# A hybrid attention and DeltaNet layer: five tiles of one merge gate instead of two behind the last heads, two fewer at the end of the attention

## The chip, the cores and the metric

The kernel runs on one NeuronCore of a Trainium2 chip. The metric is device time in microseconds (us) of one execution, smaller is better. The core's engines each work through a queue of their own: TensorE (PE in the profile; its weight loads are PEld), VectorE (DVE), ScalarE (ACT), GpSimd (POOL), and SyncE (SP), which here issues nearly all DMAs.

## The reference

One decoder layer on 512 tokens of width 2048. A normalised and modulated input `h` is projected to everything else; two branches work side by side, and a gated sum of both goes through the output projection:

```python
h = rms_norm(x, norm_w) * (1.0 + scale) + shift
proj = h @ w_in
aq, ak, av, ag, d_qkv, dz, db, da, mg_a, mg_b = jnp.split(proj, _split_points(), axis=-1)
...
a_out = swa_attention(aq, ak, av, sinks).astype(x.dtype) * jax.nn.silu(ag)
y_a = a_out @ w_o_swa
...
o = gated_delta_rule(dq, dk, dv, g, beta)
o = rms_norm(o, dn_norm_w) * jax.nn.silu(dz.reshape(B, T, DN_V_HEADS, DN_HEAD_V).astype(f32))
y_b = o.reshape(B, T, DN_VAL).astype(x.dtype) @ w_o_dn
y = jax.nn.sigmoid(mg_a) * y_a + jax.nn.sigmoid(mg_b) * y_b
return x + gate * (y @ w_out)
```

The attention has 32 query heads of 64 in 4 groups, a window of 128 and attention sinks. The DeltaNet has 32 value heads in 16 groups of two. The change is about `mg_a`, the merge gate of the attention branch: 2048 channels, which are 16 tiles of 128 channels by 512 tokens.

## The kernel before

Everything is float32, and each large product is made of three matmuls: both operands are split into a high part (`hh`, `whi`) and a low part (`hl`, `wlo`), and `mm3` (L272 to L277) adds high x high, low x high and high x low. `hh` and `hl` hold `h`, 16 tiles of 128 x 512 each, for nearly the whole program.

A *channel tile* (`channel_tile`) is one product of 128 output channels: 16 steps of three matmuls, 48 in all, over weights of 1 MB. The weights come in by an order written out by hand, `plan`: a list of jobs, one a tile, whose loads SP issues into two raw buffers (`raw`; a third for part of the time). Each raw tile is split in two halves by ScalarE (`whi`, L53) and VectorE (`wlo`, L54) into three pairs of buffers. The code must use the tiles in just the order of the list, so a tile moved in the code is moved in `plan` too.

A *merge gate* (`merge_gate`) is a channel tile, a tanh on ScalarE (`mth`, L298) and a store by SP to `ma_d` (L301). It hangs on nothing but `h`, so it can stand anywhere up to the output projection of the attention, which reads `ma_d`.

The work that hangs on long chains (a group of DeltaNet heads, a group of attention heads) is written as generators. They stand in a list `live`; every second step of a channel tile calls `pump`, which lets each generator go on when its count of pumps has run out. So the small matmuls of such a chain stand between matmuls of channel tiles, eight pumps to a tile. What is left when no tile follows is run out by `drain_live`, with nothing between.

The stages that the change touches:

- *DeltaNet heads* (`deltanet`): 16 groups, five channel tiles each. Behind the last group its scan is still in flight: four chunks one after the other (`pp`, `pv`, `pd`, `po`), then on VectorE the norm (`roy`, and `osb` at L1077), transposes `pto` on TensorE (L309), the product with the gate `zh` (L1086), stores and sums to `oq_d`. Merge gates follow, and `drain_live`.
- *DeltaNet output projection* (`branch_b`): seven products `od` of 2048 x 1024 weights, made of `oraw` tiles that are loaded from `oq_d` and split to `oh` and `ol`. Merge gates stand in front of it and behind it.
- *Attention* (`attention`): four groups of eight channel tiles, then merge gates. Each group of heads has four blocks of 128 tokens, one after the other: scores `S` (two groups of matmuls, L1413), mask and maxima on VectorE (L1419, L1424 to L1432), exponentials on ScalarE (L1437), normalisation on VectorE (L1445), transposes `pP` and copies `pT`, the product with the values `O` (L1464), the gate (`ao`, L1471) and, behind the last block of a group, a store to `ao_d`. The last group's chain runs into the merge gates.
- *Attention output projection* (`finish`): 16 channel tiles `os`. Its input takes the place of `h`: each of 16 tiles of `ao_d` is loaded by SP to `aoraw` (eight buffers, shared with the queries `aq`) and split to `hh` (ScalarE, L53) and `hl` (VectorE, L54), once the last merge gate has read that part of `h`.

The build puts each engine's instructions in a fixed order, which need not be the order of the code. An engine goes through its instructions in that order.

Of the kernel before, what the change touches and what calls it, by code (L numbers as in the profile page):

```python
# [19 lines left out]
KT = D // P  # L20
# [17 lines left out]
class Layer:  # L38
# [149 lines left out]
    def plan(self):  # L188
        a, jobs = self.a, []
        wi = lambda name, t: jobs.append((name, a["w_ch"][t]))  # L190
        jobs += [(f"st{u}", a["w_st"][u]) for u in range(KT // 2)]
        for j in range(NFIRST):
            wi(f"mb{j}", 96 + j)
        for kind, j in self.mixed():
            wi(f"{kind}{j}", (16 if kind == "k" else 96) + j)
        ma = lambda r: [wi(f"ma{j}", 146 + j) for j in r]
        ma(range(0, 3))
        for g in range(KH):
            wi(f"q{g}", g)
            for e in (2 * g, 2 * g + 1):  # L200
                wi(f"v{e}", 32 + e)
            for e in (2 * g, 2 * g + 1):
                wi(f"z{e}", 64 + e)
        ma(range(3, 5))
        ma(range(5, 7))
        for m, (name, _, w) in enumerate(self.od_order()):
            src = a["w_od"][w] if w else self.od_d[name]
            jobs += [(f"od{m}_{b}", src[b]) for b in range(8)]
        ma(range(7, 9))
        for t in range(2):  # L210
            wi(f"ak{t}", 128 + t)
        for n in range(4):
            for j in range(4):
                wi(f"aq{4 * n + j}", 112 + 4 * n + j)
            for j in range(4):
                wi(f"ag{4 * n + j}", 130 + 4 * n + j)
        ma(range(9, 16))
        jobs += [(f"os{j}", a["w_os"][j]) for j in range(KT)]
        self.jobs = jobs

# [405 lines left out]
    def deltanet(self):  # L626
# [10 lines left out]
        with ExitStack() as ps:  # L637
# [35 lines left out]
            with ExitStack() as sb:  # L673
                wk = sb.enter_context(tc.tile_pool(name="dnB", bufs=2, reuse_waits="tile"))
                self.tt = []
                for n in range(4):
                    t = wk.tile([P, NTB, P], F32, tag=f"tt{n}", name=f"tt{n}", bufs=1)
                    nc.gpsimd.memset(t[HD:P, :, 0:HD], 0.0)
                    self.tt.append(t)
                self.wmore = sb.enter_context(tc.tile_pool(name="wmore", bufs=1, reuse_waits="tile"))  # L680
                self.load_job()
                for g in range(KH):
                    if g == KH - 1:
                        self.wmore = None
                    if g == 2:
                        self.beside(self.ordered(self.od_sums()), 0.13, "ws")
                    if g == 8:
                        self.drain_slow(s1)
                        es1.close()
                        late = ps.enter_context(tc.tile_pool(name="late", bufs=1, side="right", reuse_waits="tile"))  # L690
                        self.beside(self.ordered(self.gate(late)), 0.125, "gate")
                    self.heads(wk, g)
                for j in range(3, 5):
                    self.merge_gate("ma", j, self.ma_d)
                self.drain_live()
                self.drain("ws")
                self.drain("gate")
# [419 lines left out]
    def branch_b(self):  # L1117
        tc, nc, a = self.tc, self.nc, self.a
        with ExitStack() as es:
# [14 lines left out]
            def split(u):  # L1134
                if u < 56:
                    parts[u] = [wk.tile([P, 2, 256], F32R, tag="o" + x, name="o" + x, bufs=8) for x in "hl"]
                    self.split(*parts[u], raws.pop(u))
                    load(u + 4)
# [27 lines left out]
            for j in range(3):  # L1166
                for u in (2 * j, 2 * j + 1):
                    split(u)
                if j < 2:
                    self.merge_gate("ma", 5 + j, self.ma_d)  # L1170
            for m, (name, _, _) in enumerate(order):
                ps = {}
                for kt in range(KT):
# [15 lines left out]
                    self.half_done()  # L1189
                    if kt % 2:  # L1190
                        del parts[u]
            for j in range(7, 9):
                self.merge_gate("ma", j, self.ma_d)
            self.drain_live()

# [70 lines left out]
    def attention(self):  # L1266
        tc, nc, a = self.tc, self.nc, self.a
        with ExitStack() as es:
# [33 lines left out]
                self.go(self.key_pair(wk, t, self.channel_tile(f"ak{t}"), blk, kw, kd), 0)  # L1302
            for n in range(4):
                self.group(wk, kd[n], n, blk, mask, sink, qw)
            for j in range(9, KT):
                self.merge_gate("ma", j, self.ma_d)
            self.drain("ws")
            self.drain_live()
# [466 lines left out]
```

## Time and profile before

| | us |
|---|---|
| median of 3 runs (2883.14 to 2886.53) | 2885.73 |
| the profiled execution | 2886.63 |
| its span, first to last instruction | 2884.9 |
| TensorE busy in the span | 2832.8 |
| VectorE busy | 1857.8 |
| ScalarE busy | 1139.0 |
| GpSimd busy | 272.5 |

In the profile a row of a timeline has the start (us from the span's start), the duration, the engine, the line, the operation, what it writes and reads (out<-in), the shape and the count; in brackets stands how long the engine was idle before it, and for what. Matmuls overlap, so the distance from start to start tells their pace, not the duration. In the view of waits a row has the total, the times and the longest. A row of the view by stretches gives the stretch, its length, the busy time of PE, PEld, DVE, ACT and POOL (with the count of instructions), the granted TensorE clock as a share of full speed, the DMA share and GB/s. In the chain of waits a row is the start, the duration and the work.

### The profile page before, as it was taken

How to read it: one execution, taken by the hardware profiler on the slowest of the kernel's cores; microseconds unless marked ns; L12 is line 12 of the kernel's file. 1: busy time of each engine (PE TensorE's matmuls, PEld its weight loads, DVE VectorE, ACT ScalarE, POOL GpSimd, SP SyncE). 2: the span in 40 equal slices, each digit the busy share in tenths (PEclk: the TensorE clock that was granted, in tenths of full speed). 3: DMA queues.
4: the chain of work that ended last, by engine and by line, in shares of the span. 5: the costliest groups of instructions: out<-in, count | busy, mean ns of one | idle time of the engine just before them, and what ended most of it. 6: DMA issues, size and time to landing. Idle time of an engine off the chain costs nothing.

```text
span 2884.9 us, 38287 instructions
## 1 busy us (share of the span) xinstructions
PE 2832.8 (98%) x14428; PEld 2329.4 (81%) x14428; DVE 1857.8 (64%) x3020; ACT 1139.0 (39%) x2161; POOL 272.5 (9%) x266
## 2 busy tenths in 40 slices
PE   8899999999999999999999999999999999999999
PEld 6677888888888888888887788888887788788787
DVE  6765899777776555566665456665556655554565
ACT  4354333433334333333333344443344434432343
POOL 0012121101111111111100000000100100000000
PEclk9999999999999999999999999999999999999999
DMA  9756554636767877878873477675745547365575
GB/s 381 290 171 195 180 172 156 210 109 199 226 178 216 236 227 230 260 230 242 252 202 97 133 247 265 241 252 202 224 148 163 166 147 219 119 226 181 187 237 164
DMA packets 205729, 590.08 MB, mean 205 GB/s; under 512 B 74821, under 2 KB 99909, under 8 KB 154345
## 3 DMA queue, kind: packets, MB, share of 16 engines
q1 hardware_dynamic: 195336, 529.44, 53.8%
q0 software_dynamic: 10208, 58.20, 10.4%
q8 instruction: 113, 1.85, 0.3%
q14 instruction: 72, 0.58, 0.1%
HBM read 523.79 MB, written 166.40 MB: 239 GB/s over the span
## 4 chain that ended last, share of the span: by engine, by line
PE 87%; DVE 2%; issue 2%; DMA 1%; ACT 0%; SPq 0%; POOL 0%; DVEq 0%; POOLq 0%; ACTq 0%
PE mm L275 21%; PE mm L277 20%; PE mm L276 20%; PE od L276 3%; PE od L275 3%; PE od L277 3%; PE m L276 2%; PE m L277 2%; PE m L275 2%; PE S L1413 1%; PE po L1045 1%; PE O L1464 1%; PE pv L1026 1%; PE pP L309 1%; PE po L1044 1%
## 5 line engine op out<-in xcount | busy, mean ns | idle before, releaser
L275 PE MATMUL mm<-hh,whi 128*128 128x512 f32 x2784 | 1127.4, 405 | 2.3 <-ACT whi L53 1.6
L277 PE MATMUL mm<-hh,wlo 128*128 128x512 f32 x2784 | 1089.7, 391 | 1.1 <-DVE wlo L54 1.1
L276 PE MATMUL mm<-hl,whi 128*128 128x512 f32 x2784 | 1088.8, 391 | 0.0
L54 DVE TENSOR_TENSOR wlo<-raw,whi 128x1024 fp32r<-128x1024 f32 (+1 forms) x476 | 588.8, 1240 | 464.5 <-ACT whi L53 458.5
L53 ACT CAST whi<-raw 128x1024 fp32r<-128x1024 f32 (+1 forms) x476 | 495.8, 1045 | 786.0 <-PE mm L276 665.3
L275 PEld LDWEIGHTS mm<-hh,whi 128*128 128x128 f32 x2784 | 524.6, 188 | 115.6 <-issue 9.6
L277 PEld LDWEIGHTS mm<-hh,wlo 128*128 128x128 f32 x2784 | 523.7, 188 | 114.4 <-DVE wlo L54 1.9
L276 PEld LDWEIGHTS mm<-hl,whi 128*128 128x128 f32 x2784 | 525.1, 189 | 101.8 <-issue 1.4
L276 PE MATMUL od<-wlo,oh 128*128 128x512 f32 x448 | 174.6, 390 | 0.8 <-DVE wlo L54 0.8
L275 PE MATMUL od<-whi,oh 128*128 128x512 f32 x448 | 174.9, 391 | 0.3 <-ACT whi L53 0.3
L277 PE MATMUL od<-whi,ol 128*128 128x512 f32 x448 | 174.4, 389 | 0.0
L813 POOL TENSOR_TENSOR E<-E,neg_g 128x512 f32<-128x512 f32 x64 | 79.8, 1248 | 946.6 <-DMA E<-g_rows 721.1
L865 DVE TENSOR_TENSOR A<-A,atmp 128x62 f32<-128x62 f32 (+30 forms) x124 | 112.0, 903 | 1.6
L858 DVE TENSOR_TENSOR atmp<-A 128x62 f32<-128x62 f32 (+30 forms) x124 | 110.3, 890 | 1.3
L276 PEld LDWEIGHTS od<-wlo,oh 128*128 128x128 f32 x448 | 84.1, 188 | 18.1 <-DVE wlo L54 1.1
L275 PEld LDWEIGHTS od<-whi,oh 128*128 128x128 f32 x448 | 84.1, 188 | 17.8 <-ACT whi L53 0.7
L277 PEld LDWEIGHTS od<-whi,ol 128*128 128x128 f32 x448 | 84.1, 188 | 17.7
L54 DVE TENSOR_TENSOR wlo<-raww,whi 128x1024 fp32r<-128x1024 f32 x56 | 68.4, 1222 | 44.3 <-ACT whi L53 44.3
L53 ACT CAST whi<-raww 128x1024 fp32r<-128x1024 f32 x56 | 58.9, 1054 | 79.4 <-PE m L277 71.8
L972 POOL TENSOR_TENSOR qe<-qe,yq 128x512 f32<-128x512 f32 x32 | 47.3, 1497 | 410.3 <-DMA qe<-eg_rows 346.8
L1047 ACT COPY osb<-po 128x256 f32<-128x256 f32 x64 | 23.8, 372 | 148.2 <-PE po L1045 148.2
L1437 ACT ACTIVATE sm<-sm,mx,rs 128x256 f32<-128x256 f32 (+1 forms) x128 | 71.7, 561 | 3.3 <-DVE mx L1432 3.3
(341 smaller groups left out, 3261.0 us busy)
## 6 DMA issues: line engine op xcount, KB each, us to landing
raw<-in_w_ch SPq DMA_DIRECT2D x158, 1024.0 KB
wa<-in_w_ada_ss SPq DMA_DIRECT2D x32, 1024.0 KB
od_m<-in_w_od POOLq DMA_DIRECT2D x32, 1024.0 KB, 10.7
raw<-od_m SPq DMA_DIRECT2D x32, 1024.0 KB
raw<-in_w_od SPq DMA_DIRECT2D x24, 1024.0 KB
E<-g_rows SPq DMA_DIRECT2D x64, 256.0 KB
od_m<-in_w_od SPq DMA_DIRECT2D x16, 1024.0 KB
od_m<-od_m SPq DMA_DIRECT2D x16, 1024.0 KB
```

The costliest lines, as they stand in the source:

```text
L53: self.nc.scalar.copy(out=hi, in_=src)
L54: self.nc.vector.tensor_tensor(out=lo, in0=src, in1=hi.bitcast(F32), op=ALU.subtract)
L275: nc.tensor.matmul(ps, lhsT=wh, rhs=xh, start=first, stop=False)
L276: nc.tensor.matmul(ps, lhsT=wh, rhs=xl, start=False, stop=False)
L277: self.last_mm = nc.tensor.matmul(ps, lhsT=wl, rhs=xh, start=False, stop=last).ins
L309: self.small = self.nc.tensor.transpose(dst[:, c * P : (c + 1) * P], src_cols(c), self.ident).ins.name
L813: self.in_turn(nc.gpsimd.tensor_tensor(out=E, in0=E, in1=ng, op=ALU.add))
L858: eng.tensor_tensor(out=t, in0=A[:, m : m + 1, m + 1 :].to_broadcast([P, m, n]), in1=A[:, :m, m : m + 1].to_broadcast([P, m, n]), op=ALU.mult,
L865: eng.tensor_tensor(out=A[:, :m, m + 1 :], in0=A[:, :m, m + 1 :], in1=t, op=ALU.add)
L972: self.in_turn(nc.gpsimd.tensor_tensor(out=qf, in0=qf, in1=q, op=ALU.mult))
L1026: nc.tensor.matmul(pv[:, e, :], lhsT=TT[e][:, c, :], rhs=r[:, e, :] if c else v[e][:, c, :], start=True, stop=True)
L1437: nc.scalar.activation(t, t, AF.Exp, scale=r[:, h : h + 1], bias=mx[:, h : h + 1], accum_out=den[:, h : h + 1])
```

## The change

The 16 tiles of the gate are spread otherwise over the program:

| place | tiles before | tiles after |
|---|---|---|
| in the DeltaNet's first part | 0, 1, 2 | 0, 1, 2 |
| behind the last group of heads | 3, 4 | 3 to 7 |
| in front of the DeltaNet output projection | 5, 6 | 8 |
| behind it | 7, 8 | 9, 10 |
| at the end of the attention | 9 to 15 | 11 to 15 |

In `plan` the jobs of the weights move in the same way. No work is added or left out.

```diff
@@ plan
-        ma(range(3, 5))
-        ma(range(5, 7))
+        ma(range(3, 9))
         for m, (name, _, w) in enumerate(self.od_order()):
...
-        ma(range(7, 9))
+        ma(range(9, 11))
...
-        ma(range(9, 16))
+        ma(range(11, 16))
@@ deltanet
                     self.heads(wk, g)
-                for j in range(3, 5):
+                for j in range(3, 8):
                     self.merge_gate("ma", j, self.ma_d)
                 self.drain_live()
@@ branch_b
-                if j < 2:
-                    self.merge_gate("ma", 5 + j, self.ma_d)
+                if j == 1:
+                    self.merge_gate("ma", 8, self.ma_d)
...
-            for j in range(7, 9):
+            for j in range(9, 11):
                 self.merge_gate("ma", j, self.ma_d)
             self.drain_live()
@@ attention
-            for j in range(9, KT):
+            for j in range(11, KT):
                 self.merge_gate("ma", j, self.ma_d)
```

What this does to the order on the engines is seen at two places. The lines of the changed kernel have numbers that are one lower from `plan` on.

Behind the last group of heads, VectorE before: `osb` is the norm in front of the transposes `pto`, `zh` the product that reads them, `E` the sums that are stored, `wlo` a half of weights, `ol` a part of the input of `od`.

```order
L1077 TENSOR_TENSOR osb<-osb,roy 128x512 x2
L1086 TENSOR_TENSOR zh<-pto,zh 128x512 x2
L1110 TENSOR_TENSOR E<-zh 128x256
L1106 TENSOR_TENSOR E<-zh 128x256
L1107 SCALAR_TENSOR_TENSOR E<-E,zh 128x256
L1111 SCALAR_TENSOR_TENSOR E<-E,zh 128x256
L54 TENSOR_TENSOR wlo<-raw,whi 128x1024
L54 TENSOR_TENSOR ol<-oraw,oh 128x512 x4
```

And VectorE with the change:

```order
L1076 TENSOR_TENSOR osb<-osb,roy 128x512 x2
L54 TENSOR_TENSOR wlo<-raw,whi 128x1024
L1085 TENSOR_TENSOR zh<-pto,zh 128x512 x2
L54 TENSOR_TENSOR wlo<-raw,whi 128x1024 x3
L1105 TENSOR_TENSOR E<-zh 128x256
L1106 SCALAR_TENSOR_TENSOR E<-E,zh 128x256
L1109 TENSOR_TENSOR E<-zh 128x256
L1110 SCALAR_TENSOR_TENSOR E<-E,zh 128x256
L54 TENSOR_TENSOR wlo<-raw,whi 128x1024 x2
L54 TENSOR_TENSOR ol<-oraw,oh 128x512
```

Weights of gates that were not there now stand between the norm, the product and the sums. On TensorE, 6 matmuls of a gate stand between the last scan step `po` and `pto` before, and 54 now; between `pto` and the first `od` stand 96 before and 144 now. On SP, the first four `oraw` loads stand in front of the store of the first gate that follows `pto` before, and now behind the store of gate 7.

At the end of the attention, ScalarE before: `es` and `sm` are the exponentials of the last block, `pT` copies, `mth` the tanh of a merge gate (the last one shown is that of gate 15), `hh` the high parts of the output projection's input.

```order
L1431 ACTIVATE es<-es 128x8
L1437 ACTIVATE sm,den<-sm,mx,rs 128x256 x8
L298 ACTIVATE mth<-mm 128x512
L53 CAST whi<-raw 128x1024 x2
L1455 COPY pT<-pP 128x512 x2
L53 CAST whi<-raw 128x1024
L298 ACTIVATE mth<-mm 128x512
L53 CAST hh<-aoraw 128x512 x7
L53 CAST whi<-raw 128x1024
L53 CAST hh<-aoraw 128x512 x7
L298 ACTIVATE mth<-mm 128x512
```

And ScalarE with the change (again the last `mth` is that of gate 15):

```order
L297 ACTIVATE mth<-mm 128x512
L53 CAST hh<-aoraw 128x512 x7
L53 CAST whi<-raw 128x1024
L53 CAST hh<-aoraw 128x512 x5
L1430 ACTIVATE es<-es 128x8
L1436 ACTIVATE sm,den<-sm,mx,rs 128x256 x8
L297 ACTIVATE mth<-mm 128x512
L53 CAST whi<-raw 128x1024
L1454 COPY pT<-pP 128x512 x2
L53 CAST whi<-raw 128x1024
L53 CAST hh<-aoraw 128x512 x4
```

The exponentials of the last block stood two gates ahead of the first `hh`; now twelve `hh` stand ahead of them, and the tanh of gate 15 stands behind them. On VectorE, with the change, four `hl` stand between the masks of the last block's first and second scores, and six among and behind the steps of its maxima:

```order
L54 TENSOR_TENSOR hl<-aoraw,hh 128x512 x4
L1418 TENSOR_TENSOR sm<-S,mask 128x512 x2
L1423 TENSOR_REDUCE mx<-sm 128x2 x2
L54 TENSOR_TENSOR hl<-aoraw,hh 128x512
L1426 TENSOR_TENSOR mx<-mx,rs 128x8
L54 TENSOR_TENSOR hl<-aoraw,hh 128x512
L1427 TENSOR_TENSOR mx<-mx,sink 128x8
L54 TENSOR_TENSOR hl<-aoraw,hh 128x512
L1429 TENSOR_TENSOR es<-sink,mx 128x8
L54 TENSOR_TENSOR hl<-aoraw,hh 128x512
L1431 TENSOR_SCALAR mx<-mx 128x8
L54 TENSOR_TENSOR hl<-aoraw,hh 128x512 x2
```

Before, all sixteen `hl` stand behind `ao` of the last block. On TensorE, between the second scores of the last block and its first transposes `pP`, stand 54 matmuls before (30 of gate 13 and 24 of gate 14), and a whole further gate, 48 matmuls, stands behind `O`; now 30 of gate 15 and one of the output projection stand between them. Between that matmul and `O` stand four more, one is within `O`, and behind `O` stand 30 that read the twelve tiles already split. On SP, eight `aoraw` loads stand behind the store of gate 14, then a load of weights, the store of gate 15, and only then the stores of the last group and the four loads that read them; before, the last eight loads stand behind those stores.

## The prediction

> **What bounds the kernel now.** I read the page's busy line and chain first, then the view of who waited for whom on TensorE, then the timelines around the two places where the change adds and takes cover.
>
> ```profile
> PE 2832.8 (98%) x14428; PEld 2329.4 (81%) x14428; DVE 1857.8 (64%) x3020; ACT 1139.0 (39%) x2161; POOL 272.5 (9%) x266
> PE 87%; DVE 2%; issue 2%; DMA 1%; ACT 0%; SPq 0%; POOL 0%; DVEq 0%; POOLq 0%; ACTq 0%
> ...
> PE v L275 <- ACT hh L469: 18.7, 14, 3.3
> PE pd L1041 <- DVE vs L1033: 5.7, 3, 2.5
> PE pto L309 <- DVE osb L1077: 3.7, 1, 3.7
> PE mm L275 <- ACT mth L298: 0.7, 1, 0.7
> ```
>
> TensorE is busy for 98% and makes 87% of the chain, so a merge gate costs its matmuls wherever it stands: a tile moved is worth only the TensorE waits that it covers or lays bare. In all waits there is one at each place the change touches: 3.7 us for `pto`, behind the last group of heads, and 0.7 us for `mth`, between the last merge gate and the first tile of the output projection. The sum is made against the profiled execution, 2886.63 us (its span 2884.9); the median of the runs, 2885.73, lies 0.9 below, and the forecast is given on the median.
>
> **The three tiles that move behind the heads.** TensorE there, before:
>
> ```profile
> 1635.62 0.40 PE L277 MATMUL mm<-hh,wlo 128*128 128x512 f32 x1
> 1639.75 1.32 PE L309 MATMUL pto<-ident,osb 128*128 128x128 f32 x8 [3.73 <-DVE osb L1077]
> ...
> 1641.73 0.63 PE L277 MATMUL mm<-hh,wlo 128*128 128x512 f32 x1
> 1642.15 0.63 PE L275 MATMUL mm<-hh,whi 128*128 128x512 f32 x1
> ...
> 1645.47 0.39 PE L276 MATMUL mm<-hl,whi 128*128 128x512 f32 x1
> 1645.70 0.40 PE L277 MATMUL mm<-hh,wlo 128*128 128x512 f32 x1
> ...
> 1640.93:1644.34 3.41, 3.41 (x11) 2.67 (x10) 2.39 (x6) 0.00 (x0) 0.00 (x0) 0.50 0.48 161
> 1647.75:1651.16 3.41, 3.41 (x16) 2.81 (x15) 2.11 (x3) 2.79 (x5) 0.00 (x0) 1.00 0.81 287
> ```
>
> With two gates, the transposes of the last heads stand 6 matmuls behind the last scan step and wait 3.73 us for VectorE to scale `osb`. Soon after, the granted clock is 0.50 for one stretch of 3.41 us: matmuls start 0.42 us apart there, and 0.23 us apart later. Eight start where fifteen would, so the stretch loses 7 x 0.23 = 1.6 us. In the new order 54 matmuls stand there, 12 us of work against a wait of under 4, so both go: **-3.7 and -1.6 us**. The gain's bounds are 3.7 (if the clock falls there anyway) and 5.3; I take 5.3, since nothing else idles there.
>
> The cover for the loads of the DeltaNet output projection gets thinner, because their issues on SP now stand behind the store of gate 7 and only gate 8 (48 matmuls, 11 us) is left in front of the first `od` tile:
>
> ```profile
> 1643.89 3.54 SPq L1132 DMA_DIRECT2D oraw<-oq_d  x4
> 1648.92 1.66 ACT L53 CAST oh<-oraw 128x512 fp32r<-128x512 f32 x3
> ```
>
> From the first issue to the first cast took 5.0 us there, which with 0.6 for a cast and 0.7 for its low part is under 7 us. Eleven cover it; I cost it at nothing. The two gates behind that projection stay two. The moved weight loads and gate stores are as many as before, one of each per tile.
>
> **The two tiles fewer at the end of the attention.** Here the order matters more than the count. Let s be the start of the second group of score matmuls of the last block.
>
> ```profile
> 2514.02 1.14 PE L1413 MATMUL S<-kd,aq 64*128 64x256 f32 x8
> 2515.09 0.50 PE L275 MATMUL mm<-hh,whi 128*128 128x512 f32 x1
> 2527.46 1.03 PE L309 MATMUL pP<-ident,sm 128*128 128x128 f32 x8
> 2534.79 1.97 PE L1464 MATMUL O<-pT,vtok_a 128*64 128x128 f32 x32
> 2548.60 0.50 PE L275 MATMUL mm<-hh,whi 128*128 128x512 f32 x1 [0.75 <-ACT mth L298]
> ...
> 2519.52 0.60 ACT L1437 ACTIVATE sm<-sm,mx,rs 128x256 f32<-128x256 f32 x1
> 2523.63 0.59 ACT L1437 ACTIVATE sm<-sm,mx,rs 128x256 f32<-128x256 f32 x1
> 2524.21 0.58 ACT L298 ACTIVATE mth<-mm 128x512 f32<-128x512 f32 x1
> 2537.68 4.71 ACT L53 CAST hh<-aoraw 128x512 fp32r<-128x512 f32 x7 [1.42 <-PE mm L277]
> 2542.30 1.05 ACT L53 CAST whi<-raw 128x1024 fp32r<-128x1024 f32 x1
> 2543.25 2.87 ACT L53 CAST hh<-aoraw 128x512 fp32r<-128x512 f32 x5
> ...
> 2515.18 1.29 DVE L1419 TENSOR_TENSOR sm<-S,mask 128x512 f32<-128x512 f32 x2 [1.53 <-PE S L1413]
> 2516.39 1.27 DVE L1424 TENSOR_REDUCE mx<-sm 128x2 f32<-128x512 f32 x2
> 2517.69 0.17 DVE L1427 TENSOR_TENSOR mx<-mx,rs 128x8 f32<-128x8 f32 x1
> 2524.78 2.19 DVE L1445 TENSOR_SCALAR sm<-sm,den 128x256 f32<-128x256 f32 x8
> 2526.89 1.22 DVE L54 TENSOR_TENSOR wlo<-raw,whi 128x1024 fp32r<-128x1024 f32 x1
> 2528.09 0.69 DVE L1457 COPY pT<-pP 128x512 f32<-128x512 f32 x1
> 2536.93 0.68 DVE L1471 TENSOR_TENSOR ao<-O,sg 128x512 f32<-128x512 f32 x1
> 2538.34 4.79 DVE L54 TENSOR_TENSOR hl<-aoraw,hh 128x512 fp32r<-128x512 f32 x7 [0.72 <-ACT hh L53]
> ...
> 2514.79 0.79 SPq L1312 DMA_DIRECT2D aoraw<-ao_d  x2
> 2680.94 2.00 DMA y_d<-m
> 648.03 3.60 DMA E<-g_rows
> ```
>
> Before, 54 matmuls (12.4 us, 0.229 each) lie between s+1.07 and the first transposes `pP` at s+13.4, and a whole further gate lies behind `O`. Now gate 15, the last, is under way at s: 30 of its matmuls follow, it ends at s+1.07+6.9 = s+8.0, and next in TensorE's order come one matmul of the output projection, `pP`, and `O`. The last block's softmax is bare, and it starts later, because ScalarE and VectorE now split twelve of the sixteen `aoraw` tiles ahead of it:
>
> 1. The seventh tile's buffer is one that this second group of scores reads; its load was issued at 2514.79, s+0.8. No row has that load's landing. The nearest 256 KB ones took 2.0 us (`y_d`, a store) and 3.6 (`E`, a load); I take 2.7, about midway: s+3.5.
> 2. ScalarE then casts tile 7 (0.6), one half of weights (1.05) and five tiles (2.87), and ends at s+8.0.
> 3. VectorE does masks and maxima of the first scores (4 us ahead of s), four `hl` (4 x 0.69), the masks and maxima of the second (2.5) by s+4.9, then four `hl` with four 0.17 us steps of the maxima among them (3.5): s+8.4. So the exponentials start at s+8.5, not at s+5.5 (2519.52).
> 4. They take 4.7 (2519.52 to 2524.21); the tanh of gate 15 stands behind them, 0.6: s+13.8. The first matmul of the output projection waits for that tanh, as it does at 2548.60. TensorE idles from s+8.0 to s+13.85: **5.9 us**.
> 5. The normalised `sm` were ready 7.45 us after the exponentials began (2519.52 to 2526.97): s+15.95, `pP` done at s+16.4, where without waiting it would be at s+15.0: **1.4 us**. Four matmuls later (s+17.3) the second `pP` waits until VectorE has done a `wlo` (1.22) and a copy of `pT` (0.69), about s+18.0: **0.7 us**. `O` waits for the last copies, **0.4 us**, and ends near s+21.
>
> Together 8.4 us; with the load at 2.0 or 3.6 in step 1 it is 7.7 or 9.3. Behind `O`: `ao` (0.7), a store (2.0), a load (2.7), `hh` (0.6) and `hl` (0.7) give 6.7 us, or 7.6 with the slower load, against 32 matmuls (7.3 us) that need none of it. I take **0.3 us**, bounds 0 and 2.1 (if the store too takes a load's 3.6). The 0.75 us wait of before goes: its place is inside the 5.9.
>
> The clock: an idle of 3.73 us cost one half-speed stretch above, and 5.9 will cost at least one. It falls into the restart, where about 2.3 us of TensorE work double and 1.1 us of the waits of step 5 take part of it up: **1.2 us**; bounds 0.4 (the stretch lies nearly all in the idle time) and 3.3 (two dense stretches). The Trainium skill, page "TensorE: Matmul & The Clock Gate", Part 1 on the clock gate, says that the clock halves after an idle window of about 3.4 us that runs free of the kernel, and returns only after a busy one. The 3.41 us row above agrees with that length, and by that rule the broken restart could hold the half clock longer: the total would be 2892.4 us (worked out at the second rival) where one stretch as in the row gives 2889.5.
>
> **The sum:** -3.7 - 1.6 + 8.4 + 0.3 + 1.2 - 0.75 = +3.8 us, so 2885.73 + 3.8 = **2889.5 us** (2890.4 in a profiled execution). With all bounds at their low end +1.9, at their high end +8.6.
>
> The order in the places that carry this is shown with the change. What can be told from no change is about 0.2%, 5.8 us: the three runs alone spread over 3.4 us.
>
> **The rivals.**
> - *The last group of heads comes too late for the output projection* (slower). Place: its tile 12, the first that needs `ao` of group 3. For it speaks that store and load follow each other with no other gate behind `O`; against it that the queue carries little else then. It decides once the round trip takes 1.9 us more than the 32 matmuls. At 2.1 us that bubble has a stretch of half clock of its own, 1.6 us less the 0.3 already counted: 2889.5 + 3.4 = 2892.9 us.
> - *The clock stays halved through the restart* (slower). From s+13.85 to s+21 TensorE has 5.0 us of work; doubled, less 2.5 us of waits, it adds 2.5 in place of 1.2, and one dense stretch more adds 1.6: 2892.4 us. For it speaks that the restart stops three times; against it that at 1640.93 one stretch sufficed, but work was dense there.
> - *The relief behind the heads is given back in front of `od`* (slower). If the twelve first `oraw` loads crowd each other past the 11 us, the 3 us would return: 2892.5 us. The 7 us above speak against it.
> - *The softmax is hidden after all* (faster). If the five remaining tiles cover it, only -5.3 and at most -0.75 remain: 2879.7 us. The 12.4 us that lie there before and are 6.9 now speak against it.
> - That the change moves nothing is excluded by the order.
>
> **How the numbers follow.** My forecast 0.50; late group 0.22; halved clock 0.17; relief given back 0.05; hidden softmax 0.06. Slower by over 0.2% is the three middle ones, 0.44; within 0.2% 0.50; faster 0.06. The forecast's own range is 2887.5 to 2891.5. The range of 8 in 10 takes in the bounds of the sum (+1.9 to +8.6) and a little of the faster side: 2885 to 2895.
>
> **What would show it.** The wait of `pto` for `osb` and the 0.50 stretch behind it are gone; a wait of some 6 us of the first `os` matmul for `mth` appears, with waits of `pP` and `pT` of about 1.4 and 0.7 behind it and a stretch at 0.50; exponentials of the last block start some 8.5 us after the second scores; no wait of over 1 us in front of `od`. The prediction is wrong if the first `os` matmul waits under 3 us, or if new waits outside these two places come to more than 2 us.

## The result, and the profile after

| | before | with the change |
|---|---|---|
| median (us) | 2883.62 (2879.43 to 2887.36, 22 runs) | 2887.99 (2883.65 to 2891.35, 22 runs) |
| ratio, 95% interval | | 1.0013 (1.0007 to 1.0019) |
| profiled execution, span | 2886.63, 2884.9 | 2891.35, 2889.6 |

The change costs 0.13% of 2883.62, that is 3.8 us (2.0 to 5.5 by the interval; the two medians differ by 4.4): within the 0.2% that was called no change, and by the amount that was forecast. The parts behind that amount were not all as forecast. Both profiled executions lie 3 us or more above their kernel's median.

The page of the changed kernel, busy line and chain:

```profile
PE 2832.5 (98%) x14428; PEld 2328.2 (81%) x14428; DVE 1858.2 (64%) x3020; ACT 1139.1 (39%) x2161; POOL 275.2 (10%) x266
PE 86%; DVE 2%; issue 2%; DMA 2%; ACT 1%; POOL 0%; SPq 0%; DVEq 0%; POOLq 0%; ACTq 0%
```

The busy time of TensorE is that of before (2832.8), so all of the difference is in what it waits for. The view of who waited for whom on TensorE:

```profile
PE mm L274 <- ACT mth L297: 5.7, 2, 4.3
...
PE od L275 <- DVE wlo L54: 2.4, 1, 2.4
...
PE pP L308 <- DVE sm L1444: 0.3, 1, 0.3
```

The row of `pto` is gone. Waiting for `mth` has grown from 0.7 us in one place to 5.7 in two, and the od row is new. The timeline of TensorE at the four places:

```profile
1632.49 0.39 PE L1044 MATMUL po<-vn,E 128*128 128x128 f32 x2
1645.01 1.03 PE L308 MATMUL pto<-ident,osb 128*128 128x128 f32 x8
...
1919.42 0.59 PE L275 MATMUL od<-wlo,oh 128*128 128x512 f32 x1 [2.36 <-DVE wlo L54]
...
2018.76 0.50 PE L274 MATMUL mm<-hh,whi 128*128 128x512 f32 x1 [1.41 <-ACT mth L297]
...
2533.48 1.13 PE L1412 MATMUL S<-kd,aq 64*128 64x256 f32 x8
2545.97 0.79 PE L274 MATMUL mm<-hh,whi 128*128 128x512 f32 x1 [4.34 <-ACT mth L297]
2546.56 2.23 PE L308 MATMUL pP<-ident,sm 128*128 128x128 f32 x8
2550.30 1.45 PE L308 MATMUL pP<-ident,sm 128*128 128x128 f32 x8
2552.49 1.75 PE L1463 MATMUL O<-pT,vtok_a 128*64 128x128 f32 x28
```

`pto` now has no wait. The first matmul of the output projection waits 4.34 us. The 1.41 us at 2018.76 are in front of `ak0`, the first tile of the attention, and the 2.36 us are inside the DeltaNet output projection. Neither of the last two was in the forecast.

A stop costs about 0.3 us more than the time in its brackets. Matmuls of 0.39 us start 0.23 us apart when nothing holds them, so that 0.16 us of overlap is lost at a stop, and the second matmul behind it starts 0.34 us after the first (2018.76 and 2019.10).

To see what each place is worth, the program is cut at six starts on TensorE: the last `po`, the first and the last `od`, the first `S`, the second scores of the last block (s), and the last `mm` (the end of the attention's output projection).

| start at (us) | last po | first od | last od | first S | s | last mm | span |
|---|---|---|---|---|---|---|---|
| before | 1634.36 | 1664.31 | 1975.98 | 2079.25 | 2514.02 | 2722.59 | 2884.9 |
| with the change | 1632.61 | 1678.54 | 1993.32 | 2098.29 | 2533.48 | 2726.79 | 2889.6 |
| heads_alone (below) | 1630.23 | 1654.40 | 1966.09 | 2071.06 | 2506.50 | 2715.07 | 2877.7 |

A tile takes 10.88 us: between the last `po` and the first `od` the changed kernel has six and heads_alone four, and (45.93 - 24.17) / 2 = 10.88. Taking 10.88 for every tile that moved into or out of a stretch, the difference to the kernel before is, for all profiled executions:

| us | up to last po | heads (po to od) | od | od to S | S to s | end (s to last mm) |
|---|---|---|---|---|---|---|
| with the change | -1.8 | -5.8 | +3.1 | +1.7 | +0.4 | +6.5 |
| heads_alone | -4.1 | -5.8 | 0.0 | +1.7 | +0.7 | 0.0 |
| end_alone | -3.5 | 0.0 | +0.1 | 0.0 | +1.4 | +6.8 |
| two_in_front | -6.8 | -5.8 | -0.2 | 0.0 | +1.9 | +6.4 |
| other_bank | -0.7 | -5.8 | -0.3 | +1.7 | +1.0 | +5.9 |
| skipped_buffer | -1.5 | -5.8 | +0.2 | +1.8 | +0.2 | +6.1 |
| late_splits | -4.1 | -5.8 | -0.4 | +1.7 | +2.0 | +6.8 |
| all_late | -6.6 | -5.8 | -0.7 | +1.7 | +0.7 | +2.6 |
| six_at_end | -6.9 | -5.8 | +0.3 | 0.0 | +0.6 | +2.3 |
| four_at_end | -2.1 | -5.8 | -0.4 | 0.0 | +1.0 | +13.1 |
| none_behind | -1.8 | -5.8 | +0.3 | +10.0 | +2.5 | 0.0 |

The first column is a part of the program in which nothing was moved, and it differs by up to 6.9 us from one execution to the next. The stretch from the first `S` to s has the same order on TensorE in nearly all these kernels and still differs by up to 2.0 us (in none_behind it has a wait of its own, below; in four_at_end 18 matmuls of gates stand behind s instead of ahead of it, and are taken into account). Behind the last `mm` each took 0.2 to 1.1 us longer than the kernel before did. So one profile's span says little about a change of 4 us, and the times below are medians of many runs, while the columns tell where the time goes. What belongs to the change is -5.8, +1.7 and +6.5, together +2.4 us; the executions below with the same order at the end put the last term at 5.9 to 6.8.

### The profile page after: what moved, and what is told of

Its sections match the earlier page's. It is cut to its first block, busy times and chain, and to the rows that moved or that the text cites. A ratio compares the mean times of both kernels' runs of the same rounds, so it can differ in the third digit from the quotient of the medians.

```text
span 2889.6 us, 38283 instructions
## 1 busy us (share of the span) xinstructions
PE 2832.5 (98%) x14428; PEld 2328.2 (81%) x14428; DVE 1858.2 (64%) x3020; ACT 1139.1 (39%) x2161; POOL 275.2 (10%) x266
## 3 DMA queue, kind: packets, MB, share of 16 engines
q8 instruction: 113, 1.85, 0.3%
## 4 chain that ended last, share of the span: by engine, by line
PE 86%; DVE 2%; issue 2%; DMA 2%; ACT 1%; POOL 0%; SPq 0%; DVEq 0%; POOLq 0%; ACTq 0%
PE mm L274 20%; PE mm L276 20%; PE mm L275 20%; PE od L275 3%; PE od L276 3%; PE od L274 3%; PE m L275 2%; PE m L276 2%; PE m L274 2%; PE S L1412 1%; PE po L1044 1%; PE pP L308 1%; PE pv L1025 1%; PE O L1463 1%; PE po L1043 1%
```

## The experiments

All spread the thirteen movable tiles otherwise, or change one thing in the changed kernel. "3, 1, 2, 7" are the tiles behind the last heads, in front of the DeltaNet output projection, behind it, and at the end of the attention; the kernel before is 2, 2, 2, 7 and the change 5, 1, 2, 5. Unless one says so, the order of the weights' loads follows.

### Each half of the change alone

heads_alone, 3, 1, 2, 7 (against the changed kernel):

```diff
-                for j in range(3, 8):
+                for j in range(3, 6):
-                    self.merge_gate("ma", 8, self.ma_d)
+                    self.merge_gate("ma", 6, self.ma_d)
-            for j in range(9, 11):
+            for j in range(7, 9):
-            for j in range(11, KT):
+            for j in range(9, KT):
```

> The change's half at the heads alone: three tiles behind the last heads, one in front of the DeltaNet output projection, two behind it, seven at the end as in the kernel before. Theory 'the heads' gain is real': no wait of pto for osb, no half-clock stretch behind it, 5.3 us less than the kernel before from these two. If the wait of the first attention tile ak0 for mth (1.4 us in the changed kernel) comes from the count of tiles in front of it, it is here again, since the count between heads and attention is that of the changed kernel, and the net is about -4 us. Rival 'the gain is taken back in the output projection': the wait of od for wlo (2.4 us, 4 with its half-clock stretch) is here too, the net is about 0. In the last block the order is that of before: first os matmul waits about 0.75 us.

end_alone, 2, 2, 4, 5: the loops at the heads and in front of `od` as in the kernel before, `range(7, 11)` behind it, `range(11, KT)` at the end.

> The change's half at the end of the attention alone: two and two tiles around the heads as in the kernel before, four behind the DeltaNet output projection, five at the end. Theory 'the bare softmax costs it': pto waits 3.7 us with its half-clock stretch as before, the first os matmul waits 4.3 to 5.9 us for mth, the whole 6.5 (by the changed kernel's trace) to 9.2 us (by the prediction's sum) slower than the kernel before. Rival 'the loss lies elsewhere, in od and ak0': at most 4 us slower. No wait of ak0, if that hangs on the count of tiles in front of it (34 here, 31 in the changed kernel).

Measured: heads_alone 2879.57 us against 2885.5 before, ratio 0.9983 (0.9974 to 0.9991), 4.9 us less; end_alone 2891.72, ratio 1.0023 (1.0013 to 1.0033), 6.6 us more. Together they make +1.7, the change +3.8: the intervals of each part are 2 to 3 us to either side, and the sum lies inside them. TensorE in heads_alone, the last `po` and the first `od`, with as many tiles between them as before:

```profile
1630.11 0.39 PE L1044 MATMUL po<-vn,E 128*128 128x128 f32 x2
...
1654.40 0.39 PE L274 MATMUL od<-whi,oh 128*128 128x512 f32 x1
```

And the same two in the kernel before:

```profile
1634.25 0.39 PE L1045 MATMUL po<-vn,E 128*128 128x128 f32 x2
...
1664.31 0.39 PE L275 MATMUL od<-whi,oh 128*128 128x512 f32 x1
```

30.06 us before and 24.29 here: 5.8 us, the wait of `pto` (3.73), what a stop costs beyond that, and the half-clock stretch behind it (1.6). The same 5.8 stand in every execution that has three or more tiles behind the heads. The gain at the heads is real, and the loss is at the end of the attention. heads_alone also has the wait of `ak0` (1.41 us), and no long wait of `od` (0.97); its time is below both kernels.

### What od and ak0 wait for

two_in_front, 4, 2, 2, 5: `range(3, 7)` behind the heads, gates 7 and 8 in front of `od`.

> The changed kernel with four tiles behind the heads and two in front of the DeltaNet output projection, in place of five and one. TensorE's order is the same, instruction by instruction; what differs is which PSUM buffer each tile has and when the oraw tiles are loaded and split. Theory 'ak0 waits because its PSUM buffer is that of the last gate': the wait of 1.4 us goes. If the wait of od for wlo (2.4 us) is due to the split order in front of od, it goes as well: together 1.5 to 5.5 us less than the changed kernel; if it is an accident of one execution, only 1.4. Rival 'neither hangs on this': the time of the changed kernel, within 1 us. The end of the attention as in the changed kernel.

other_bank:

```diff
-            self.pmm = es.enter_context(tc.tile_pool(name="pmma", bufs=2, space=PSUM, reuse_waits="tile"))
+            self.pmm = es.enter_context(tc.tile_pool(name="pmma", bufs=2, space=PSUM, reuse_waits="tile")); self.pmm.tile([P, T], F32, tag="mm", name="skip")
```

> The changed kernel, every engine's order the same, but one PSUM buffer of the attention's pool is given out and not used, so that each tile there takes the other of the two buffers: ak0 not that of the last gate in front of it, and the first tile of the output projection not that of gate 15. Theory 'the softmax chain sets the end, the tanh only shows it': the wait of ak0 goes (1.4 us), the first os matmul doesn't wait for mth, but the transposes pP right behind it wait about 4.3 us for sm instead; 1 to 2 us less than the changed kernel. Rival 'the tanh that stands behind the exponentials is the cause': the 4.3 us go as well, and 5 to 7 us are gained with the clock's stretches.

In other_bank the buffer that was given out and not used came back at once: in the built program every tile of it has the PSUM buffer that it has in the changed kernel. So it answers nothing about buffers, and is a second look at the changed kernel: 2886.75 us, ratio 1.0012 (1.0003 to 1.0020), a wait of `od` of 0.94 us in place of 2.36, and the same waits at the other places. The 3.1 us in `od` are thus an accident of the one profiled execution; none of the eleven others has them. VectorE, in the changed kernel:

```profile
1917.55 0.69 DVE L1213 SCALAR_TENSOR_TENSOR yb<-bth,pty 128x512 f32<-128x512 f32 x1 [5.47 <-DMA yb_d<-yb]
```

The halves of weights `wlo` that `od` waits for stand right behind this `yb`, and it waited 5.47 us for a store of an earlier `yb`, where the eleven others wait 3.3 to 4.3 us. That execution lies 3.4 us above its kernel's median.

two_in_front: 2887.49 us, ratio 1.0009 (1.0000 to 1.0018). The wait of `ak0` is gone, as expected, and the end costs what it did. The time to the changed kernel differs by less than the intervals tell apart.

To move the buffers in earnest, skipped_buffer writes the skipped buffer once:

```diff
             self.pmm = es.enter_context(tc.tile_pool(name="pmma", bufs=2, space=PSUM, reuse_waits="tile"))
+            skip = self.pmm.tile([P, T], F32, tag="mm", name="skip")
+            nc.tensor.transpose(skip[:, 0:P], self.ident, self.ident)
```

> The changed kernel with one transpose of 128x128 into a PSUM buffer of the attention's pool ahead of its first tile, never read, so that every tile there takes the other of the two buffers; the orders else are the same, but for one half of weights on ScalarE and VectorE near ak0. Theory 'the softmax chain sets the end, the tanh only shows it': the wait of ak0 (1.4 us) is gone, and the first os matmul no longer waits for mth (4.3 us), but pP, one matmul behind it, waits about 4.4 us for sm; 1 to 2 us less than the changed kernel. Rival 'the tanh behind the exponentials is the cause': the 4.3 us go too, 5 to 7 us less.

Measured 2886.82 us, ratio 1.0012 (1.0003 to 1.0021): as slow as the change. Its waits on TensorE:

```profile
PE pP L308 <- DVE sm L1446: 4.7, 2, 4.5
...
PE skip L1270 <- ACT mth L297: 1.4, 1, 1.4
```

Both waits have changed their owner. The 1.4 us in front of `ak0` now belong to the transpose that took `ak0`'s buffer, so it is the buffer that waits, and whoever comes first to it. In the built program the last gate behind `od` has PSUM buffer 0, that of `ak0`, in each kernel with one tile in front of `od` (the change, heads_alone, other_bank, skipped_buffer, late_splits, all_late), and another one where two stand in front and two or four behind; the wait is there in the first and not in the others. The Trainium skill, page "Perfetto Trace Analysis", section "Optimizing Tensor Performance", says that independent groups of matmuls should rotate through different PSUM banks, so that emptying one lies beside the matmuls of the next; the 1.41 us are what it costs here where a pool's end and the next pool's start meet on the same one.

At the end of the attention the first matmul of the output projection no longer waits for the tanh of gate 15. But the transposes `pP`, one matmul later in TensorE's order, wait 4.5 us for `sm`. The softmax of the last block sets the time there; the tanh only stands last in the same queue. From s to the last `mm` it costs 6.1 us against 6.5.

### Why the exponentials start late

The changed kernel, ScalarE and VectorE behind the second scores of the last block (s = 2533.48):

```profile
2535.54 0.62 ACT L53 CAST hh<-aoraw 128x512 fp32r<-128x512 f32 x1 [1.34 <-PE mm L276]
...
2538.85 1.25 ACT L53 CAST hh<-aoraw 128x512 fp32r<-128x512 f32 x2 [0.17 <-DMA aoraw<-ao_d]
...
2540.66 0.61 ACT L1436 ACTIVATE sm<-sm,mx,rs 128x256 f32<-128x256 f32 x1 [0.45 <-DVE mx L1431]
...
2545.35 0.57 ACT L297 ACTIVATE mth<-mm 128x512 f32<-128x512 f32 x1
...
2533.03 2.49 DVE L54 TENSOR_TENSOR hl<-aoraw,hh 128x512 fp32r<-128x512 f32 x4
2535.43 1.28 DVE L1418 TENSOR_TENSOR sm<-S,mask 128x512 f32<-128x512 f32 x2
2536.63 1.27 DVE L1423 TENSOR_REDUCE mx<-sm 128x2 f32<-128x512 f32 x2
2537.82 0.68 DVE L54 TENSOR_TENSOR hl<-aoraw,hh 128x512 fp32r<-128x512 f32 x1
...
2540.45 0.17 DVE L1431 TENSOR_SCALAR mx<-mx 128x8 f32<-128x8 f32 x1
```

The second scores were done at 2534.61, but VectorE was busy with four `hl` until 2535.43, and four more stand among the small steps of the maxima. The exponentials start at s + 7.2, against s + 5.5 in the kernel before. late_splits puts the casts of five tiles behind them (`last_exp` is the last of the exponentials):

```diff
+                n = len(nc.cur_bb.bb.instructions)
                 self.split(self.hh[:, kt, :], self.hl[:, kt, :], raw)
+                for i in nc.cur_bb.bb.instructions[n:] if 7 <= kt < 12 else []:
+                    if i.engine == mybir.EngineType.Activation:
+                        self.tc.add_manual_dep(i, self.last_exp.name, ...)
```

> The changed kernel with the casts of the tiles 7 to 11 of the output projection's input behind the last exponentials on ScalarE, in place of in front of them. Theory of the prediction 'the splits delay the exponentials by 3 us': they start 5.5 us after the second scores instead of 7.2 (8.5 in the prediction), the tanh of gate 15 ends 1.7 us earlier, and the wait of the first os matmul falls from 4.3 to 2.6 us. Rival 'the splits stand in idle time and cost nothing': the exponentials start within 0.3 us of 7.2, the wait stays 4.3. The transposes pP are now mixed with matmuls of the output projection that need the late casts, so that part of the gain can be lost behind them; the whole time 0 to 2 us less than the changed kernel.

Measured 2887.79 us, ratio 1.0012 (1.0004 to 1.0021). The exponentials start at s + 6.7 and the wait is 3.9 us: not 5.5 and 2.6. ScalarE was free and waited for VectorE (2.91 us, for `es`), where five `hl` still stood among masks and maxima. Nothing is won by it: 6.8 us at the end against 6.5. So the second form moves all but the first two tiles (`2 <= kt < 12`):

> As late_splits, but with the casts of the tiles 2 to 11 behind the last exponentials, so that hardly any hl split stands among the last block's masks and maxima on VectorE. Theory 'what delayed the exponentials is the hl splits on VectorE, not the casts on ScalarE': they start 5.5 us after the second scores, as in the kernel before (6.7 in late_splits, 7.2 in the changed kernel), and the first os matmul waits for mth about 2.7 us. Rival 'something else of the new order holds them': 6.5 us or more. What is won can be lost again behind pP, since the matmuls there need the late casts; the whole time within 2 us of the changed kernel.

Measured 2882.22 us, ratio 0.9993 (0.9984 to 1.0002), where the changed kernel had 1.0013. Its second scores start at 2525.17; then:

```profile
2526.33 1.29 DVE L1425 TENSOR_TENSOR sm<-S,mask 128x512 f32<-128x512 f32 x2 [1.53 <-PE S L1419]
2530.66 0.60 ACT L1443 ACTIVATE sm<-sm,mx,rs 128x256 f32<-128x256 f32 x1
...
2535.98 0.50 PE L274 MATMUL mm<-hh,whi 128*128 128x512 f32 x1 [2.66 <-ACT mth L297]
```

VectorE takes the masks as soon as the scores are there, the exponentials start at s + 5.5, and TensorE waits 2.66 us: as expected to 0.1 us. The end costs 2.6 us in place of 6.5. Of the 3.9 us, 1.7 are the shorter wait (2.66 in place of 4.34), and no stretch at half clock follows it. So the splits on VectorE in front of the softmax, together with the half clock that the longer wait brings, are more than half of the loss (the transposes `pP` also stand between other matmuls in this kernel, so that the 3.9 us are not of the splits alone). The first form did not show it: it freed ScalarE, but VectorE still held the exponentials back.

### How many tiles the end needs

six_at_end, 3, 2, 2, 6, and four_at_end, 5, 2, 2, 4:

> Three tiles behind the last heads, two in front of the DeltaNet output projection, two behind it, six at the end. In TensorE's order 54 matmuls stand between the last scan step and pto, as in the changed kernel, and 54 between the second scores of the last block and pP, as in the kernel before. Theory 'both places only need their cover': no wait of pto (-5.3 us), no wait of ak0 (the last gate has another PSUM buffer than ak0), no wait of the first os matmul for mth either (0.75 us in the kernel before; six tiles put gate 15 into the other buffer): about 5 to 6 us less than the kernel before, 2.5 less than the changed kernel's gain alone would need. Rival 'each tile fewer at the end costs half of the 6.5 us': 2 us less than before at most.

> Five tiles behind the last heads, two in front of the DeltaNet output projection, two behind it, four at the end. In TensorE's order both scores of the last block now stand ahead of the whole of gate 15, and its 48 matmuls and five of the output projection (53, 12 us) lie between them and the first pP; in the changed kernel 31 do. Theory 'what counts is how many matmuls stand behind the last scores, not how many tiles are left': no wait over 1.5 us at the first os matmul or pP, the heads' 5.3 us are kept, and what is lost is behind O (the load of the last heads' ao against fewer than 32 matmuls, 1 to 3 us): 2 to 4 us less than the kernel before. Rival 'each tile fewer lays more of the softmax bare': 5 to 10 us more is lost than with five, the whole 6 to 12 us slower than the kernel before.

Measured: six 2881.18 us, ratio 0.9990 (0.9981 to 0.9998), 2.8 us less than before; four 2891.95, ratio 1.0031 (1.0019 to 1.0043), 9 more. Both expectations on waits at the softmax hold: with six tiles neither the first `os` matmul nor `pP` waits for `mth` or `sm`, and with four they do not either. (With an even number of tiles at the end the built program gives gate 15 and the first `os` tile different PSUM buffers, so that this tile can't wait for that tanh; that `pP` does not wait either is what shows the softmax covered.) The times do not hold, since something else takes their place; with four the rival's time came out, but not for its reason. TensorE with six tiles, and then with four, there with ScalarE and SP:

```profile
2547.09 0.73 PE L274 MATMUL mm<-hh,whi 128*128 128x512 f32 x2 [0.81 <-ACT hh L53]
2549.86 0.50 PE L274 MATMUL mm<-hh,whi 128*128 128x512 f32 x1 [0.39 <-ACT hh L53]
...
2551.77 0.50 PE L274 MATMUL mm<-hh,whi 128*128 128x512 f32 x1 [0.46 <-ACT hh L53]
```

```profile
2538.07 1.13 PE L1412 MATMUL S<-kd,aq 64*128 64x256 f32 x4 [1.79 <-DVE sm L1418]
...
2564.24 0.63 PE L274 MATMUL mm<-hh,whi 128*128 128x512 f32 x1 [3.80 <-ACT hh L53]
2574.57 0.71 PE L274 MATMUL mm<-hh,whi 128*128 128x512 f32 x1 [2.77 <-DVE m L1495]
...
2563.57 1.30 ACT L53 CAST hh<-aoraw 128x512 fp32r<-128x512 f32 x2 [7.73 <-DMA aoraw<-ao_d]
2558.46 1.78 SPq L1472 DMA_DIRECT2D ao_d<-ao  x4
2560.57 2.65 SPq L1311 DMA_DIRECT2D aoraw<-ao_d  x4
```

With four, 53 matmuls cover the softmax and five of them are already the output projection's, but behind `O` only 11 are left that need no `ao` of the last heads. The way from the first store to the first cast takes 5.1 us (2558.46 to 2563.57), and TensorE stands still for 3.80. In the changed kernel that way is as long, 5.25 us, but 30 matmuls, 6.8 us of work, stand behind `O` there:

```profile
2555.00 1.78 SPq L1472 DMA_DIRECT2D ao_d<-ao  x4
2560.25 0.62 ACT L53 CAST hh<-aoraw 128x512 fp32r<-128x512 f32 x1 [0.84 <-DMA aoraw<-ao_d]
```

This is the mechanism of the prediction's rival "the last group of heads comes too late". The 2.77 us are for `m`, the sum that empties the PSUM buffer of the first output tile: VectorE does it at 2573.84, right behind a half of weights that it took at 2572.69. So the number of tiles alone does not tell the cost: five lay the softmax bare, four the way back of its result.

Six cost 2.3 us at the end. The rows above, with 0.23 us for an `hl` at 2550.58, are four stops of 1.9 us; one of 0.75 is saved at `mth`. With 0.3 us more for each stop that makes 2.0, and 0.3 are open. Here too it is the way back through memory:

```profile
2536.80 0.33 SPq L234 DMA_DIRECT2D raw<-in_w_os  x1
2537.40 2.30 SPq L1472 DMA_DIRECT2D ao_d<-ao  x4
2543.66 2.20 SPq L1311 DMA_DIRECT2D aoraw<-ao_d  x4
```

The loads go 6.3 us after the first store, where it took 2.1 us in the changed kernel (2555.00 to 2557.10). A load of 1 MB of weights was issued 0.6 us ahead of these stores; that it held them up is not shown by a run.

none_behind, 4, 2, 0, 7, to win the wait of `ak0` back as well:

> Four tiles behind the last heads, two in front of the DeltaNet output projection, none behind it, seven at the end: the heads' gain with the end of the kernel before, and no gate whose PSUM buffer ak0 would have to wait for. Theory 'the two tiles behind the DeltaNet output projection cover nothing': no wait of pto, about 1.4 us less than with heads_alone, 5 to 7 us less than the kernel before. Rival 'they cover the last sums of that projection and the first loads of the attention': a new wait of 2 to 10 us at ak0 or ptva, so that the whole is the kernel before's time or slower.

Measured 2890.23 us, ratio 1.0017 (1.0008 to 1.0026). The rival was right in size, but the wait stands at another place, `kss`, the matmul that sums the squares of the first keys:

```profile
2021.34 0.63 ACT L1250 ACTIVATE cos<-ang 128x512 f32<-128x512 f32 x1 [3.72 <-DVE ang L1239]
2022.51 2.07 PE L1330 MATMUL kss<-ksq,blk 128*128 128x512 f32 x2 [5.79 <-ACT ksq L1325]
2088.18 0.49 PE L1412 MATMUL S<-kd,aq 64*128 64x128 f32 x4 [1.25 <-DVE aq L1263]
```

The two tiles behind the DeltaNet output projection cover the angles of the attention's sine and cosine tables. VectorE computes them until 2021.31, ScalarE waits 3.72 us for them, and the squares `ksq` that `kss` reads stand behind the cosine. With 6.83 us at half clock from 2021.40 on, the stretch up to the first `S` costs 10.0 us. The quickest of all the kernels is heads_alone, 0.9983 of before, though its interval overlaps with those of six_at_end and all_late. A kernel that has it all (three tiles behind the heads, seven at the end, and no shared buffer at `ak0`) was not run.

## Why the prediction was right in sum, and where not

- **The sum**, +3.8 us: measured +3.8 (2.0 to 5.5). That they agree to a tenth is luck. The end was put 2.65 us too high, `ak0` (1.7) was missing, and the heads won 0.5 more: the parts that belong to the change add up to +2.4, which the interval takes in. The forecast of 2889.5 us lies 1.5 above the measured 2887.99, since it starts from 2885.73 for the kernel before, whose median is 2883.62 over 22 runs. The bounds of the sum are added up wrongly: by the terms' own bounds they are +2.05 and +10.25, not +1.9 and +8.6 (the upper one leaves out that the heads might win only 3.7), and a store of 3.6 us brings the tail to 1.9, not 2.1.
- **The heads**, -3.7 and -1.6: right; -5.8 in place of -5.3, and the same in every execution with that cover. About 0.3 of the rest is what a stop costs beyond its brackets. The thinner cover in front of `od` costs nothing, as said: no wait there. The rival "relief given back" falls.
- **The end of the attention**, 8.4 + 0.3 + 1.2 - 0.75 = 9.15: the mechanism was right, the size was not. In the profiled execution it is 6.5, in the five with this order on TensorE 5.9 to 6.8. The term that was mis-sized is step 4, the wait of 5.9 us, which measured 4.34 (4.33 to 4.74 in the others). It goes back to steps 1 to 3, where the exponentials were put at s + 8.5 and came at s + 7.2. The seventh tile was cast at s + 2.1, held by TensorE and not by its load, where step 1 took s + 3.5. And eight `hl` were charged 0.69 us each, the duration of one alone, where four in a row take 2.49. That the splits delay the exponentials was the point on which the step rested; all_late shows it.
- **Step 5 and the clock**: the waits of 1.4, 0.7 and 0.4 us do not show, because matmuls at half clock fill that time. From the first `os` matmul to the end of `O` it took 8.27 us (2545.97 to 2554.24), where the steps and the clock's 1.2 us came to 8.35. Whether one or two windows of 3.41 us were halved, the rival's question, turned out either way in executions of the same order: one in other_bank and skipped_buffer, which lost 5.9 and 6.1 us at the end, two in the change, end_alone and two_in_front, which lost 6.5, 6.8 and 6.4. So the rival's condition was met, but the second window cost about half a microsecond, where the rival's time lay 2.9 above the forecast.
- **The tail behind O**, 0.3: no wait on TensorE. It became one as soon as the softmax was covered (six_at_end) or fewer matmuls were left (four_at_end).
- **What was missed**: `ak0`, +1.7. The step "the two gates behind that projection stay two" looked at their number and order, and not at which PSUM buffer the last of them gets. One tile fewer in front of `od` shifts it.
- The prediction named a sum of new waits elsewhere of over 2 us as a sign that it was wrong. In the profiled execution they are 2.36 and 1.41, so by that sign it was. 1.41 of it belongs to the change; the other is that execution's own.

## What to carry to other kernels

A tile of independent work is worth what the stretch it leaves had under it, to be looked up for each stretch by itself: here the softmax, the way back of its result through memory, and the angles of the next stage each needed their cover, and the change left only the softmax too little of it. When work gets less room in front of a chain's last step, look at all the engines of that chain for what a scheduler now lets pass ahead of it; holding back what is not yet needed won more than half of the loss here, at no cost in cover. And a tile moved out of a pool's sequence can move the PSUM buffer at the next pool's start, which no order of instructions shows.

## What the runs showed of the hardware that was not expected

The granted clock goes by a fixed grid of 3.41 us, and half a window is enough. In the twelve profiled executions all stretches at half clock behind 200 us start on one grid of 3.413 us within their execution. Measuring for each window of that grid how long no matmul ran (up to 8 us before the end), each of the 29 drops came right behind a window with 1.70 us or more of idle. Of the windows at full clock with so much idle only two, with 1.77 and 1.84, had no drop behind them. The clock came back behind a halved window with at most 0.25 us of idle, and stayed down behind the five with 0.87 or more. In the first 200 us, where the work is another, the edge is less sharp: five drops came behind 1.50 to 1.52 us of idle, windows with up to 1.93 had none, and the clock came back behind 0.46 and stayed down behind 0.56. The view by stretches of the changed kernel at `od` and at the end of the attention, window by window:

```profile
1916.27:1919.68 3.41, 0.85 (x3) 0.45 (x3) 2.13 (x3) 1.70 (x3) 0.00 (x0) 1.00 0.52 203
1919.68:1923.09 3.41, 3.41 (x9) 2.63 (x9) 1.53 (x3) 1.04 (x1) 0.00 (x0) 0.50 0.84 228
...
2540.91:2544.32 3.41, 0.73 (x4) 0.26 (x2) 2.04 (x3) 3.41 (x13) 0.00 (x0) 1.00 0.17 22
2544.32:2547.74 3.42, 1.77 (x6) 1.05 (x6) 2.20 (x9) 2.54 (x6) 0.00 (x0) 0.50 0.84 341
2547.74:2551.15 3.41, 3.41 (x13) 2.76 (x12) 2.10 (x4) 0.59 (x1) 0.00 (x0) 0.50 0.06 21
```

And of all_late, whose longer wait of 2.66 us falls on both sides of an edge:

```profile
2531.40:2534.81 3.41, 1.92 (x9) 1.27 (x7) 0.00 (x0) 3.41 (x13) 0.00 (x0) 1.00 0.66 274
2534.81:2538.23 3.42, 2.25 (x13) 1.83 (x14) 2.68 (x11) 3.42 (x9) 0.00 (x0) 1.00 0.20 77
```

A wait of 2.36 us inside one window (busy 0.85) halves the next; one of 2.66 us, 1.49 before the edge and 1.17 behind it, does not. By the windows behind 200 us, a single wait under 1.7 us has no such price, one of over 3.7 leaves 1.85 in some window and has it, and between them the place in the grid decides. The Trainium skill, page "TensorE: Matmul & The Clock Gate", Part 1, gives a window of 3413 ns that runs free of the kernel, which agrees with the grid, and an idle window as the condition of the halving: here half of one was enough.
